# Four rounded weight blocks parked in DRAM: moving the splitting of the first right factors of a down projection into the attention part

## The chip, the cores and the metric

One core of a Trainium2 chip runs one launch of the kernel. The metric is the device time of that launch in microseconds (us), as a median over runs. A profiled execution gives the trace; its span is the time from its first to its last instruction on the engines.

## The reference

One encoder layer over 512 tokens of width 2048, all in float32:

```python
h = rms_norm(x, pre_mix_g);   z = h @ w_in                  # q | k | v | u
a = chunked_attention(q, k, v, rel_bias)                    # 8 heads of 128
p = multiscale_pool(u, pool_w, pool_scale)
x = x + rms_norm(concat(a, p) @ w_o, post_mix_g)
h = rms_norm(x, pre_ffn_g)
up = causal_dwconv(h @ w_up, conv_w, conv_b)                # w_up: 2048 x 2*5632
y = (gelu(up[..., :5632]) * up[..., 5632:]) @ w_down        # w_down: 5632 x 2048
x = x + rms_norm(y, post_ffn_g)
```

## The kernel before

**Numbers.** TensorE (PE) multiplies in a rounded format, fp32r. A factor that must be exact to more than that is *split*: ScalarE (ACT) writes a rounded copy, the high part (`hi`, L136), and VectorE (DVE) writes what is left, the low part (`lo`, L137). A product is then three matmuls, hi x hi, lo x hi and hi x lo (`mm3`, L152, L154, L155). In the trace `bh`, `bl` are the parts of a right factor, `ah`, `al` those of a left one, `p` the products.

**Stages.** The mixing part (queries, keys and values head by head, attention, pooling, `w_o`) takes the first third of the span. Weights come there through `load_w`, called by `Weights`: a raw tile from a ring of five (`raw4`), split into a pair from a ring of eight (`w4`, so four pairs), four blocks ahead of their use. `specs` is the list of blocks in the order of use. For each head h from 2 to 7 the loop does `head("q", h)`, `turn(h - 2)`, `scores(h - 1)`, `head("k", h)`, `values(h - 2)`. Between these steps `sums_in_dram` copies and adds blocks of `w_o` and `w_down` in DRAM (L284, L287), since both products are done by a seven-product scheme (Strassen's in Winograd's form) that multiplies sums of blocks.

Then comes the up projection, 22 pairs of column blocks (`u` from 0 to 21), the last 19 of them also with seven products each (`seven`, names `qa`, `qg`, `qd`). After each, DVE and ACT combine the products (`keep`, `keep_all`), apply the convolution (`taps`), the gelu (`gate`) and the product of the two halves (`product`), and the result goes to DRAM as `gd` (L916, L918), by a DMA that GpSimd (POOL) issues. `factors.order` fixes the order of the products; its end is written out by hand.

Last comes the down projection in five chunks plus a rest. A product there takes a right factor of 512 rows by 512 columns out of `w_down` or of a sum of its blocks, and a left factor out of `gd`: `multiply` issues 4 x 2 x 3 = 24 matmuls. The seven products are numbered 1 to 7 and each is done for two column halves, `cc` 0 and 1. For chunk 0 the order is `ORDER0`: (0,1), (1,1), (0,2), (1,2), then 5, 6, 3, 7, 4 for both halves.

**The passage.** So is called here the change from the up to the down projection. `right(c, cc)` is a generator that gives the split right factor of each product. In chunk 0 it loads one block (`first_right`, L845, issued by SyncE, SP; the names are `t` in the trace), from `w_down` for products 1, 2 and 3, from the sums in DRAM for the others, and splits it. `next_first` calls it for (0,1) and (1,1) while the up projection still runs; `factors()` (the second one, in the last part) gives all others, with their left factors (`left`, `gc` in the trace, L1197), and runs three products ahead of `multiply` (`AHEAD`).

The tiles of right factors are of 8 KB per partition. The first two of each kind (`right_tile`, tags `raw1`, `wh`, `wl`) lie in a pool `pr`, opened in place of the sums `h5`, `h3`, `h6`, which the last products of the up projection read. Later ones lie in a pool `p4` that takes the place of the up projection's tiles; the loop of `r("place")` fixes which ring lies where. A tile waits for the last reader of what lay there before.

**Order on the engines.** The order on PE is the program's own (`manual_schedule`). On ACT, DVE, POOL and SP a scheduler orders the instructions when the program is built, and then every engine takes them strictly in that order. `tc.issue_after(x)` places an instruction behind x.

Of the kernel before, what the change touches and what calls it, by code (L numbers as in the profile page):

```python
# [9 lines left out]
F32 = mybir.dt.float32  # L10
# [5 lines left out]
P = 128  # L16
S = 512
# [29 lines left out]
def f32(ap):  # L47
    return ap.bitcast(F32)
# [28 lines left out]
def encoder_layer(ctx: ExitStack, tc: tile.TileContext, x, xT, vecs, rel, post_mix, post_ffn,  # L77
# [56 lines left out]
    def split(hi, lo, src, scale=None):  # L134
        if scale is None:
            rounded = nc.scalar.activation(hi, src, AF.Copy)  # L136
            nc.vector.tensor_sub(lo, src, f32(hi))  # L137
        else:
            rounded = nc.scalar.activation(hi, src, AF.Copy, scale=scale)
            nc.vector.scalar_tensor_tensor(lo, src, scale, f32(hi), op0=ALU.mult, op1=ALU.subtract)  # L140
        split.last = rounded.ins
        return rounded.ins

    def load_w(name, src, a, b):
# [98 lines left out]
    def wo_specs(i, cc):  # L243
# [2 lines left out]
        return [(f"wo{i}_{cc}_{k}", whole[:, sl, :], 2, 512)  # L246
                for k, sl in enumerate(parts)]

    specs = v_specs(0)
    for h in range(1, HEADS):  # L250
        q, k = qk_specs(h)
        specs += q + k
        if h == 5:
            specs += v_specs(1)
    for g in range(4):
        for j in range(2):
            specs += halves(f"u{2 * g + j}", w_in, head_cols("u", 2 * g + j), 8, P)
        if g:
            specs += pm_spec(g - 1)
# [12 lines left out]


    first_sum = {i: [dram.tile([P, CU, S], F32, name=f"t{i}{cc}") for cc in range(2)] for i in (5, 7, 6, 4)}

    def first_block(cc, j, l):
        cs = slice(l * D // 2 + cc * S, l * D // 2 + (cc + 1) * S)
        return w_down[:2 * P * CU, cs].rearrange("(u j p) n -> p u j n", j=2, p=P)[:, :, j, :]

    def sums_in_dram():  # L280

# [61 lines left out]
    with tc.tile_pool(name="p1", bufs=2, reuse_waits="tile") as p1:  # L343
# [175 lines left out]
        for h in range(2, HEADS):  # L519
            head("q", h)  # L520
            next(sums_step)
            turn(h - 2)
            scores(h - 1)
            next(sums_step)
            head("k", h)
            next(sums_step)
            if h == 5:
                v_keep(1, v_group(1, lambda: values(3)))
            else:
                values(h - 2)  # L530
            next(sums_step)
        next(sums_step)
        pool_proj(0, 0)
# [274 lines left out]
    def right(c, cc):  # L808

        def load(j, l):  # L810
            b = later["raw2"](f"b{j}{l}") if j else raw1(f"b{j}{l}")
            r, cs = 256 * CU * c, slice(l * C + cc * S, l * C + (cc + 1) * S)
            nc.sync.dma_start(b, w_down[r:r + 256 * CU, cs].rearrange(
                "(u j p) n -> p u j n", j=2, p=P)[:, :, j, :])
            return b

        b = {}
        order = yield
        while True:
            i = order  # L820
            if c == 0:

                v = first_right(cc, i, raw1 if ORDER0.index((cc, i)) % 5 < 3 else later["raw2"])
            else:
                for jl in {1: (11, 12), 7: (22,), 2: (21,)}.get(i, ()):
                    b[jl] = load(jl // 10 - 1, jl % 10 - 1)
                if i == 5:
                    nc.vector.tensor_add(b[11], b[11], b[12])  # L828
                if i == 7:
                    nc.vector.tensor_add(b[12], b[22], b[12])  # L830
                if i == 6:
                    nc.vector.tensor_add(b[11], b[11], b[22])
                if i == 4:
                    nc.vector.tensor_add(b[21], b[21], b[11])
                v = b[{1: 11, 5: 11, 7: 12, 6: 11, 2: 21, 3: 22, 4: 21}[i]]
            hi, lo = right_tile("wh", "bh"), right_tile("wl", "bl")
            split(hi, lo, v)
            order = yield hi, lo

    def first_right(cc, i, ring):  # L840

        v = ring(f"t{i}")
        source = first_sum[i][cc] if i in first_sum else first_block(cc, *{1: (0, 0), 2: (1, 0), 3: (1, 1)}[i])
        with tc.issue_after(first_right.last) if first_right.last else nullcontext():
            first_right.last = nc.sync.dma_start(v, source).ins  # L845
        return v

    first_right.last = None

    ORDER = 1, 5, 7, 6, 2, 3, 4  # L850

# [36 lines left out]
    with tc.tile_pool(name="p3", bufs=2, reuse_waits="tile") as p3:  # L888
# [19 lines left out]

        def product(u, g, z):
            for j in range(2):  # L910
                c = p3.tile([P, S], F32, tag="cb", bufs=1, name="cb")
                taps(z[:, j, :], KF + 2 * u + j, c)
                nc.vector.tensor_mul(g[:, j, :], g[:, j, :], c)
            if u < NC * CU:
                for i in range(2):
                    nc.gpsimd.dma_start(gd[u // CU][i][:, u % CU, :, :], g[:, :, i * H:(i + 1) * H])  # L916
            else:
                nc.gpsimd.dma_start(gd_last[u - NC * CU], g)  # L918
# [85 lines left out]
        class Factors:  # L1004
# [20 lines left out]
            def load(self, k, i):  # L1025
                def raw(what, tile_, m, kh):
                    nc.sync.dma_start(tile_, self.block(k, m, kh))
                    self.raw[k, what] = tile_

                if i == 1:  # L1030
                    raw("w" if k in self.alone else "x", raw_x("wx"), 0, 0)
                elif i == 5 and k in self.alone:
                    raw("x", raw_x("wx"), 0, 0)
                    self.late.append((self.loaded + (2 if k else 0), k))
                elif i == 3:
                    raw("y", raw4("wy"), 1, 1)
                elif i == 2:
                    raw("z", raw4("wz"), 0, 1)
# [51 lines left out]
        def keep(k, i):  # L1090

            if i == 1:
                zs[k, "1"] = pair_tile("za", 1, 2)
                nc.scalar.activation(wide(zs[k, "1"]), banks[k, "a"], AF.Copy)
            elif i == 2:
                v = wide(zs[k, "1"])
                nc.vector.tensor_add(v, banks.pop((k, "d")), v)
            elif i == 5:
                zs[k, "5"] = raw_x("zb")[:, :S] if k == end else wide(pair_tile("zb", 1))
                nc.scalar.activation(zs[k, "5"], banks[k, "g"], AF.Copy)  # L1100
            elif i == 6:
                zs[k, "m"] = pair_tile("zm", 2)
                v = wide(zs[k, "m"][:, :1])
                nc.scalar.activation(v, banks[k, "a"], AF.Copy)  # L1104
                nc.vector.tensor_add(v, banks.pop((k, "g")), v)
            elif i == 7:
                v = wide(zs[k, "m"][:, 1:])
                keep.copied = nc.scalar.activation(v, banks[k, "a"], AF.Copy).ins
                nc.vector.tensor_add(v, zs.pop((k, "5")), v)
            elif i == 4:  # L1110
                keep_all(k)
# [50 lines left out]
        for k, i in factors.order:  # L1162
            seven(k, i)
            keep(k, i)
            if (k, i) == (end, 6):
                summed.close()
                pr = ctx.enter_context(tc.tile_pool(name="pr", bufs=2, side="right", reuse_waits="tile"))
            if (k, i) == (end, 6):
                next_first()
            elif (k, i) == (end, 7):  # L1170
                with tc.issue_after(keep.copied):
                    next_first()
        firsts = [multiply(l, r) for l, r in firsts]
    phase.close()

    with tc.tile_pool(name="p4", bufs=2, reuse_waits="tile") as p4:
# [10 lines left out]

        for r in (later["wh"], product_part, later["raw1"], half_g, raw2, later["wl"], slot_h, slot_l, scratch):  # L1190
            r("place")

        def left(c):

# [26 lines left out]
                i = yield hi, lo  # L1221

        def factors():
            nonlocal right_split
            for c in range(NC):
                ls, made = left(c), {}
                next(ls)
                rs = rights
                if c:
                    rs = [right(c, cc) for cc in range(2)]  # L1230
                    for r in rs:
                        next(r)
                order = [(cc, i) for cc, o in ((0, ORDER), (1, LAST if c == NC - 1 else ORDER)) for i in o]
                for cc, i in order if c else ORDER0[2:]:
                    r = rs[cc].send(i)
                    right_split = split.last
                    if i not in made:
                        made[i] = ls.send(i)
                    yield c, cc, i, made[i], r

        ready, right_split = [], None

        def next_product():
            c, cc, i, l, r = ready.pop(0)
# [2 lines left out]
        for f in factors():  # L1247
            ready.append(f)
            if firsts:
                with tc.issue_after(right_split), tc.issue_after(split.last):  # L1250
                    for cc, ps in enumerate(firsts):
                        keep_product(0, cc, 1, ps)
                firsts = ()
# [167 lines left out]
```

## Time and profile before

| what | value |
|---|---|
| time, median of 3 runs | 1887.79 us (1887.65 to 1889.65) |
| profiled execution, its own time | 1887.05 us |
| its span | 1885.0 us |
| PE busy | 1868.4 us, 99% of the span |
| DVE busy | 1423.7 us, 76% |
| ACT busy | 989.2 us, 52% |
| DMA | 410.24 MB, 218 GB/s over the span |
| end of the last up product on PE | about 1446 us after the start of the span |

In the views, a row of the timeline reads: start in us, length in us, engine, line, operation, out<-in, shapes, count; in brackets the idle time of the engine just before it and what ended that. A row of the waits reads: who waited for whom, us in total, times, longest. A row of the stretches reads: stretch, length, and for each engine the busy time with its number of instructions, then the granted clock of PE, the busy share of the 16 DMA engines and what they moved in GB/s. Ends of matmuls are modelled, and matmuls overlap: the distance of their starts tells their rate. Some matmul records are missing.

### The profile page before, as it was taken

The page shows a single profiled execution, that of the slowest core. Times are in us where ns is not written, and L with a number is a line of the kernel's source. Part 1 is how long each engine was busy: PE and PEld are TensorE (multiplying, and loading weights), DVE is VectorE, ACT ScalarE, POOL GpSimd, SP SyncE. Part 2 cuts the span into 40 slices and gives each one's busy share as a digit, 9 for nine tenths or more (in the row PEclk, how much of TensorE's full clock was granted, in tenths as well). Part 3 has the DMA queues.
Part 4 walks back from the last instruction along what each step waited for, and adds up shares of the span by engine and source line. Part 5 has one row for each costly group of instructions (what it writes and reads, how often), then busy time and mean ns, then how long its engine had stood idle before and what let it go on. Part 6 is the DMA issues. An engine that isn't in the chain of part 4 may idle for free.

```text
span 1885.0 us, 24700 instructions
## 1 busy us (share of the span) xinstructions
PE 1868.4 (99%) x9438; PEld 1594.3 (85%) x9438; DVE 1423.7 (76%) x1616; ACT 989.2 (52%) x1238; POOL 313.6 (17%) x403
## 2 busy tenths in 40 slices
PE   9999999999999999999999999999999999999998
PEld 7888888888888888888888888888887888888886
DVE  5454445587598667888888888888878799898877
ACT  6333233346465345656566566665656665465543
POOL 5101011000000102221222212122121122222221
PEclk9999999999999999999999999999999999999999
DMA  7599299359796848888888888888887999999998
GB/s 250 161 249 240 87 281 228 102 153 330 233 305 218 228 146 198 199 207 211 194 204 197 208 205 200 207 197 203 203 187 227 350 262 250 241 226 234 223 224 240
DMA packets 188230, 410.24 MB, mean 218 GB/s; under 512 B 11536, under 2 KB 62608, under 8 KB 183568
## 3 DMA queue, kind: packets, MB, share of 16 engines
q0 software_dynamic: 56384, 155.21, 44.0%
q1 hardware_dynamic: 131728, 253.46, 39.1%
q8 instruction: 74, 1.21, 0.3%
q14 instruction: 44, 0.36, 0.1%
HBM read 352.00 MB, written 106.95 MB: 243 GB/s over the span
## 4 chain that ended last, share of the span: by engine, by line
PE 94%; DVE 2%; DMA 1%; ACT 1%; issue 1%; SPq 0%; POOL 0%; POOLq 0%; DVEq 0%; ACTq 0%
PE qa L160 14%; PE qa L166 7%; PE qg L160 7%; PE p L155 6%; PE p L152 6%; PE p L154 6%; PE qg L166 4%; PE qd L160 3%; PE m L155 3%; PE m L152 3%; PE m L154 3%; PE up L154 2%; PE up L155 2%; PE up L152 2%; PE qd L166 2%; PE u L152 2%
## 5 line engine op out<-in xcount | busy, mean ns | idle before, releaser
L160 PE MATMUL qa<-gT,wfh 128*128 128x512 f32 x912 | 228.3, 392 | 0.0
L137 DVE TENSOR_TENSOR wfl<-wx,wfh 128x1024 fp32r<-128x1024 f32 x152 | 185.9, 1223 | 55.0 <-ACT wfh L136 40.1
L136 ACT ACTIVATE wfh<-wx 128x1024 fp32r<-128x1024 f32 x152 | 161.1, 1060 | 121.7 <-PE qg L160 46.4
L152 PE MATMUL p<-bh,ah 128*128 128x512 f32 x560 | 218.4, 390 | 1.3 <-ACT ah L136 1.3
L155 PE MATMUL p<-bh,al 128*128 128x512 f32 x560 | 218.7, 391 | 1.0 <-DVE al L137 1.0
L154 PE MATMUL p<-bl,ah 128*128 128x512 f32 x560 | 218.4, 390 | 1.2 <-DVE bl L137 1.2
L160 PEld LDWEIGHTS qa<-gT,wfh 128*128 128x128 f32 x912 | 164.1, 189 | 29.4
L1041 POOL DMA_DIRECT2D wx<-in_w_up x114 | 98.5, 864 | 452.8 <-DVE wfl L137 441.9
L160 PE MATMUL qg<-h,wfh 128*128 128x512 f32 x608 | 150.2, 389 | 0.0
L136 ACT ACTIVATE bh<-b 128x2048 fp32r<-128x2048 f32 x56 | 106.9, 1917 | 60.0 <-DVE b L828 39.3
L137 DVE TENSOR_TENSOR bl<-b,bh 128x2048 fp32r<-128x2048 f32 x56 | 127.6, 2287 | 9.0 <-PE p L154 8.0
L160 PEld LDWEIGHTS qg<-h,wfh 128*128 128x128 f32 x608 | 114.0, 188 | 23.5
L136 ACT ACTIVATE wfh<-wy 128x1024 fp32r<-128x1024 f32 x76 | 80.5, 1060 | 94.1 <-PE qg L160 46.2
L166 PE MATMUL qa<-gT,wfl 128*128 128x256 f32 x912 | 127.7, 283 | 1.2 <-ACT zm L1104 1.2
L155 PEld LDWEIGHTS p<-bh,al 128*128 128x128 f32 x560 | 105.5, 188 | 23.8 <-DVE al L137 1.8
L152 PEld LDWEIGHTS p<-bh,ah 128*128 128x128 f32 x560 | 105.5, 188 | 23.5 <-ACT ah L136 1.7
L154 PEld LDWEIGHTS p<-bl,ah 128*128 128x128 f32 x560 | 105.4, 188 | 23.3 <-DVE bl L137 1.6
L166 PEld LDWEIGHTS qa<-gT,wfl 128*128 128x128 f32 x912 | 119.9, 191 | 4.7 <-ACT zm L1104 1.6
L883 POOL DMA_DIRECT2D sum<-part x60 | 71.4, 1209 | 253.3 <-DVE part L874 114.3
L137 DVE TENSOR_TENSOR wfl<-wy,wfh 128x1024 fp32r<-128x1024 f32 x76 | 92.8, 1221 | 8.6 <-ACT wfh L136 4.7
L137 DVE TENSOR_TENSOR wfl<-wz,wfh 128x1024 fp32r<-128x1024 f32 x38 | 46.6, 1227 | 56.1 <-PE qa L160 51.9
L166 PEld LDWEIGHTS qg<-h,wfl 128*128 128x128 f32 x608 | 82.9, 190 | 5.9
(500 smaller groups left out, 4320.2 us busy)
## 6 DMA issues: line engine op xcount, KB each, us to landing
wx<-in_w_up POOLq DMA_DIRECT2D x114, 512.0 KB, 6.1
sum<-part POOLq DMA_DIRECT2D x70, 512.0 KB, 8.7
b<-in_w_down SPq DMA_DIRECT2D x32, 1024.0 KB, 9.3
wx<-in_w_up SPq DMA_DIRECT2D x40, 512.0 KB, 5.4
wz<-in_w_up SPq DMA_DIRECT2D x38, 512.0 KB, 5.7
wy<-in_w_up SPq DMA_DIRECT2D x38, 512.0 KB, 4.6
wy<-in_w_up POOLq DMA_DIRECT2D x38, 512.0 KB, 6.7
wt<-in_w_o POOLq DMA_DIRECT2D x16, 1024.0 KB, 11.5
```

The source lines that it names most:

```text
L136: rounded = nc.scalar.activation(hi, src, AF.Copy)
L137: nc.vector.tensor_sub(lo, src, f32(hi))
L152: nc.tensor.matmul(ps, l[0], r[0], start=first, stop=False)
L154: nc.tensor.matmul(low, l[0], r[1], start=False, stop=False)
L155: nc.tensor.matmul(ps, l[1], r[0], start=False, stop=last)
L160: nc.tensor.matmul(ps, w[0][:, kb], pairs[kb][0], start=fresh and not kb, stop=last, skip_group_check=not fresh)
L166: nc.tensor.matmul(ps[:, sl], w[1][:, kb], pair[:, sl], start=False, stop=last, skip_group_check=not fresh)
L883: nc.gpsimd.dma_start(dest, v, accum_op=ALU.add)
L1041: nc.gpsimd.dma_start(self.raw[k, what], self.block(k, m, kh), accum_op=ALU.add)
```

## The change

The right factors of the first four products of the down projection, (0,1), (1,1), (0,2) and (1,2), are plain blocks of `w_down`. They are now loaded and split in the mixing part, in heads 2, 3, 4 and 6, as two more blocks of 128 x 1024 in `specs` for each factor, and their high and low parts are written to DRAM by SP. At the passage `right` no longer loads and splits these four; POOL loads the two parts from DRAM straight into the tiles. The rest of the change orders the passage: the second of these requests is made earlier, the places of the rings in `p4` change, the splits for products 5 and 6 are placed behind the first left split, and the last `product` uses a second scratch tile (`cx`), so that its two halves no longer share one.

```diff
@@ split
-            nc.vector.tensor_sub(lo, src, f32(hi))
+            rest = nc.vector.tensor_sub(lo, src, f32(hi))
...
-        split.last = rounded.ins
+        split.last, split.rest = rounded.ins, rest.ins
@@ encoder_layer
+    READY = {2: (0, 1), 3: (1, 1), 4: (0, 2), 6: (1, 2)}
+    ready_w = {at: [dram.tile([P, CU, S], F32, name=f"rw{at[0]}{at[1]}{p}") for p in "hl"] for at in READY.values()}
+
+    def ready_specs(h):
+        if h not in READY:
+            return []
+        cc, i = READY[h]
+        return [(f"rw{cc}{i}_{j}", first_block(cc, i - 1, 0)[:, 2 * j:2 * j + 2, :], 2, 512) for j in range(CU // 2)]
+
     specs = v_specs(0)
     for h in range(1, HEADS):
         q, k = qk_specs(h)
         specs += q + k
         if h == 5:
             specs += v_specs(1)
+        specs += ready_specs(h)
@@ the loop over heads
                 values(h - 2)
+            for j in range(CU // 2 if h in READY else 0):
+                cc, i = READY[h]
+                for dest, v in zip(ready_w[cc, i], weights.get(f"rw{cc}{i}_{j}")):
+                    nc.sync.dma_start(dest[:, 2 * j:2 * j + 2, :], f32(v))
             next(sums_step)
@@ right
             i = order
+            if (c, (cc, i)) in ready_first:
+                hi, lo = right_tile("wh", "bh"), right_tile("wl", "bl")
+                for v, source in zip((hi, lo), ready_w[cc, i]):
+                    nc.gpsimd.dma_start(v, source.bitcast(F32R))
+                order = yield hi, lo
+                continue
             if c == 0:
-                v = first_right(cc, i, raw1 if ORDER0.index((cc, i)) % 5 < 3 else later["raw2"])
+                v = first_right(cc, i, raw1 if (ORDER0.index((cc, i)) - len(ready_first)) % 5 < 3 else later["raw2"])
@@ first_right
-        source = first_sum[i][cc] if i in first_sum else first_block(cc, *{1: (0, 0), 2: (1, 0), 3: (1, 1)}[i])
+        source = first_sum[i][cc] if i in first_sum else first_block(cc, 1, 1)
...
+    ready_first = [(0, at) for at in READY.values()]
@@ product
-                c = p3.tile([P, S], F32, tag="cb", bufs=1, name="cb")
+                if u == NU - 1 and j:
+                    c = raw_x("cx")[:, :S]
+                else:
+                    c = p3.tile([P, S], F32, tag="cb", bufs=1, name="cb")
@@ Factors.load
-                    self.late.append((self.loaded + (2 if k else 0), k))
+                    self.late.append((self.loaded + (3 if k else 0), k))
@@ the loop over factors.order
             if (k, i) == (end, 6):
                 next_first()
-            elif (k, i) == (end, 7):
-                with tc.issue_after(keep.copied):
-                    next_first()
+            elif (k, i) == (end - 1, 4):
+                next_first()
@@ the places of p4
-        for r in (later["wh"], product_part, later["raw1"], half_g, raw2, later["wl"], slot_h, slot_l, scratch):
+        for r in (product_part, later["raw1"], later["wh"], half_g, raw2, later["wl"], slot_h, slot_l, scratch):
             r("place")
+        for _ in range(3):
+            slot_l("place")
@@ factors
-                    r = rs[cc].send(i)
-                    right_split = split.last
+                    with ExitStack() as behind:
+                        if c == 0 and i in (5, 6):
+                            for ins in first_split:
+                                behind.enter_context(tc.issue_after(ins))
+                        r = rs[cc].send(i)
+                    if (c, cc, i) == (0, 1, 2):
+                        first_split = split.last, split.rest
...
             if firsts:
-                with tc.issue_after(right_split), tc.issue_after(split.last):
+                with tc.issue_after(split.last):
                     for cc, ps in enumerate(firsts):
                         keep_product(0, cc, 1, ps)
```

In the built program the order on PE is the same before and after, matmul for matmul. On POOL the end of the order is now: the last additions to `wx`, the next to last `gd`, high and low part of (0,1), high and low part of (1,1), the low part of (1,2), the last `gd`, high and low part of (0,2), the high part of (1,2), and then the writes of the products' sums. The low part of (1,2) has the tile of the low part of (0,1), and so waits for the second to last matmul of the first product; the other three tiles are free before the up projection's last product. On SP the passage now has: the sums for (0,5) and (1,5), the two `gc` blocks, the sums for (0,6) and (1,6), the block for (0,3), and so on.

More of the change, by code (lines that the diff above doesn't have):

```diff
@@ L136, in split @@
             rounded = nc.scalar.activation(hi, src, AF.Copy)
-            nc.vector.tensor_sub(lo, src, f32(hi))
+            rest = nc.vector.tensor_sub(lo, src, f32(hi))
         else:
             rounded = nc.scalar.activation(hi, src, AF.Copy, scale=scale)
-            nc.vector.scalar_tensor_tensor(lo, src, scale, f32(hi), op0=ALU.mult, op1=ALU.subtract)
-        split.last = rounded.ins
+            rest = nc.vector.scalar_tensor_tensor(lo, src, scale, f32(hi), op0=ALU.mult, op1=ALU.subtract)
+        split.last, split.rest = rounded.ins, rest.ins
         return rounded.ins
@@ L247, in wo_specs, with first_block @@
                 for k, sl in enumerate(parts)]
+    def first_block(cc, j, l):
+        cs = slice(l * D // 2 + cc * S, l * D // 2 + (cc + 1) * S)
+        return w_down[:2 * P * CU, cs].rearrange("(u j p) n -> p u j n", j=2, p=P)[:, :, j, :]
+    READY = {2: (0, 1), 3: (1, 1), 4: (0, 2), 6: (1, 2)}
[5 more added lines that the diff above has]
+        return [(f"rw{cc}{i}_{j}", first_block(cc, i - 1, 0)[:, 2 * j:2 * j + 2, :], 2, 512) for j in range(CU // 2)]
     specs = v_specs(0)
@@ L274, in encoder_layer @@
     first_sum = {i: [dram.tile([P, CU, S], F32, name=f"t{i}{cc}") for cc in range(2)] for i in (5, 7, 6, 4)}
-    def first_block(cc, j, l):
-        cs = slice(l * D // 2 + cc * S, l * D // 2 + (cc + 1) * S)
-        return w_down[:2 * P * CU, cs].rearrange("(u j p) n -> p u j n", j=2, p=P)[:, :, j, :]
     def sums_in_dram():
@@ L1107, in keep @@
                 v = wide(zs[k, "m"][:, 1:])
-                keep.copied = nc.scalar.activation(v, banks[k, "a"], AF.Copy).ins
+                nc.scalar.activation(v, banks[k, "a"], AF.Copy)
                 nc.vector.tensor_add(v, zs.pop((k, "5")), v)
@@ L1223, in factors @@
         def factors():
-            nonlocal right_split
             for c in range(NC):
@@ L1239, in factors @@
                     yield c, cc, i, made[i], r
-        ready, right_split = [], None
+        ready = []
         def next_product():
```

## The prediction

> **What bounds the kernel now.** First the page's busy times, then the same by stage.
>
> ```profile
> PE 1868.4 (99%) x9438; PEld 1594.3 (85%) x9438; DVE 1423.7 (76%) x1616; ACT 989.2 (52%) x1238; POOL 313.6 (17%) x403
> ...
> 100.00:350.00 250.00, 250.00 (x1193) 210.73 (x1192) 122.77 (x232) 83.49 (x153) 21.46 (x47) 1.00 0.80 209
> ...
> 1490.00:1860.00 370.00, 370.00 (x1634) 306.46 (x1633) 323.98 (x231) 195.95 (x189) 77.56 (x67) 1.00 0.97 244
> ```
>
> PE is the bound: idle for 16.6 of 1885 us, never in the heads (100 to 350 us) and never in the down projection behind the passage (1490 to 1860). So work spared on ACT or DVE is worth nothing except where PE waits for it, and a stall added is paid in full. The waits of PE show where it waits in the passage, and its timeline shows how much is lost there:
>
> ```profile
> PE p L152 <- ACT ah L136: 1.3, 1, 1.3
> PE p L154 <- DVE bl L137: 1.2, 1, 1.2
> PE p L155 <- DVE al L137: 1.0, 2, 0.6
> ...
> 1445.94 0.39 PE L152 MATMUL p<-bh,ah 128*128 128x512 f32 x1
> ...
> 1456.59 0.39 PE L155 MATMUL p<-bh,al 128*128 128x512 f32 x1
> 1458.30 0.50 PE L152 MATMUL p<-bh,ah 128*128 128x512 f32 x1 [1.32 <-ACT ah L136]
> 1460.05 0.50 PE L154 MATMUL p<-bl,ah 128*128 128x512 f32 x1 [1.25 <-DVE bl L137]
> 1461.19 0.80 PE L155 MATMUL p<-bh,al 128*128 128x512 f32 x1 [0.63 <-DVE al L137]
> ...
> 1464.22 0.39 PE L152 MATMUL p<-bh,ah 128*128 128x512 f32 x1
> ...
> 1474.66 0.39 PE L154 MATMUL p<-bl,ah 128*128 128x512 f32 x1
> ```
>
> The first down product starts at 1445.94. From there to 1456.59 are 47 steps (two products of 24 matmuls), 0.2266 us each. The matmul at 1474.66 is the second in the second triple of the fifth product, so 4 x 24 + 4 = 100 steps from the start: undisturbed it would stand at 1445.94 + 22.66 = 1468.60. **The passage loses 6.06 us.** That is all that the change can win; what follows runs without a gap.
>
> **What it removes.** Two groups of rows carry the passage on the two helpers:
>
> ```profile
> 1440.57 2.29 DVE L137 TENSOR_TENSOR bl<-t,bh 128x2048 fp32r<-128x2048 f32 x1
> ...
> 1450.21 1.23 DVE L1120 TENSOR_TENSOR z<-z,RR 128x1024 f32<-128x1024 f32 x1
> 1452.32 0.75 DVE L893 SCALAR_TENSOR_TENSOR cb<-z,vec,cb 128x511 f32<-128x511 f32 x1 [0.89 <-ACT cb L892]
> ...
> 1457.10 0.69 DVE L913 TENSOR_TENSOR ca<-ca,cb 128x512 f32<-128x512 f32 x1
> ...
> 1446.56 0.36 ACT L1118 ACTIVATE z<-qa 128x256 f32<-128x256 f32 x1
> 1451.47 0.82 ACT L892 ACTIVATE cb<-z,vec 128x512 f32<-128x512 f32 x1 [4.54 <-DVE z L1120]
> 1455.40 1.90 ACT L136 ACTIVATE bh<-t 128x2048 fp32r<-128x2048 f32 x1
> ```
>
> Four splits go: 4 x 1.90 on ACT, 4 x 2.29 on DVE. Two of DVE's stand ahead of the last `z` (1450.21), so `z` can start right behind ACT's copy, at 1446.92. Then `z` 1.23, the first `cb` 0.82, and on DVE, with `cx` so that the halves overlap, 4 x 0.75 + 2 x 0.69: the last product of halves ends at 1446.92 + 1.23 + 0.82 + 3.00 + 1.38 = 1453.35, against 1457.79 now. By itself this would free the third product's left factor in time, and the 6 us with it.
>
> **What it adds at the passage.** The third and fourth product now wait for POOL's queue. Its rows, and SP's:
>
> ```profile
> 1427.11 0.57 POOL L918 DMA_DIRECT2D gd<-ca  x1 [0.42 <-DVE z L1116]
> 1458.35 0.55 POOL L918 DMA_DIRECT2D gd<-ca  x1 [30.67 <-ACT ah L136]
> 1459.50 0.72 POOL L885 DMA_DIRECT2D sum<-part  x1 [0.61 <-ACT part L878]
> ...
> 1446.13 0.34 SPq L1197 DMA_DIRECT2D gc<-gd  x1
> 1446.57 0.37 SPq L845 DMA_DIRECT2D t<-in_w_down  x1
> 1447.05 0.44 SPq L845 DMA_DIRECT2D t<-t  x1
> 1447.58 0.51 SPq L1197 DMA_DIRECT2D gc<-gd  x1
> 1448.19 0.92 SPq L845 DMA_DIRECT2D t<-t  x2
> ```
>
> POOL issues the loads for (0,1) and (1,1) behind the `gd` of 1427.11, from 1427.7 on: their tiles are free by then, and the first product starts 18 us later. The next in POOL's order, the low part of (1,2), waits for the first product's end, 1451.4, and behind it stands the last `gd`, which cannot go before 1453.35 + 0.56 (the distance from DVE's end at 1457.79 to 1458.35 now) = 1453.9. Only then comes the high part of (0,2). With 0.55 for `gd` and 0.72 for a load, (0,2) is requested at 1454.5 (high) and 1455.2 (low). Its tiles have been free since 1440; it waits in line. The third product should start at 1445.94 + 48 x 0.2266 = 1456.82, and its second matmul reads the low part.
>
> When do these parts land? The page of SP's requests, each of 1 MB:
>
> ```profile
> DMA to landing us min/median/max: 4.9/4.9/4.9
> DMA to landing us min/median/max: 8.3/13.9/19.2
> ...
> 1457.00:1461.00 4.00, 1.01 (x2) 0.37 (x2) 3.97 (x4) 4.00 (x7) 1.78 (x3) 0.96 1.01 426
> q1 hardware_dynamic: 222, 1.56, 74.1%
> q0 software_dynamic: 149, 0.55, 26.8%
> ```
>
> The first line is the `gc` of 1446.13, which found the DMA engines empty. The second is the four `t` issued right behind it, up to 1448.67: they land up to 19.2 us after issue, one after the other, with the engines full (share 1.01 at 426 GB/s in the third line). The last two are SP's and POOL's queue from 1461 to 1466 us: they share those engines, 74% and 27%. The changed kernel still sends 5 MB on SP's queue at 1446 to 1448 (two `gc`, two `t` for product 6, one for product 3). On POOL's queue, ahead of the end of (0,2)'s low part, come the low part of (1,2), `gd`, and the two parts: 1.05 + 0.52 + 2 x 1.05 = 3.67 MB. Together 8.9 MB; 1.3 of them are through by 1451 (251 GB/s in 1446 to 1451, as now), the rest takes 7.6 / 0.426 = 18 us: 1469. Bounds: alone on the engines from 1454.5, (0,2)'s high part lands after 4.9 and the low part 2.5 (1.05 MB at 426) later, 1462; with a quarter of the engines until SP is through, 1475. I take 1469.5, as both queues are known to be full then.
>
> So the third product's second matmul comes at 1469.5 instead of 1457.05: 12.5 us. The clock adds to it: after the pause now, 1461.19 to 1464.22 holds 8 steps in place of 13.4, 1.2 us lost, and I take 1.7 after a longer one. Then (1,2)'s high part (3 us behind) and the splits for product 5 are ready, since DVE and ACT had the pause for them. Loss 14.2 in place of 6.06: **+8.1 us at the passage**, and nothing behind it gives that back.
>
> The Trainium skill speaks against the change here: "DMA: Bandwidth & Descriptors", section "Issuing engines are not separate DMA queues", says that a second issuing engine brings no bandwidth, as all use the same 16 DMA engines. The two shares above, 101% together, agree.
>
> **What it adds in the heads.** Eight loads and 16 writes of 0.5 MB, and 8 splits. Prices, from the page and the DMA view of 95 to 135 us:
>
> ```profile
> L137 DVE TENSOR_TENSOR wfl<-wx,wfh 128x1024 fp32r<-128x1024 f32 x152 | 185.9, 1223 | 55.0 <-ACT wfh L136 40.1
> L136 ACT ACTIVATE wfh<-wx 128x1024 fp32r<-128x1024 f32 x152 | 161.1, 1060 | 121.7 <-PE qg L160 46.4
> k_0r<-in_w_in SPq DMA_DIRECT2D x1, 512.0 KB, 16.7
> ```
>
> DVE gets 8 x 1.22 = 9.8 us more in stretches where it is busy half of the time, ACT 8.5. A load stands five raw tiles and four pairs, nine blocks, ahead of its use. With six blocks a head instead of four, that is 1.5 heads; the two projections of a head alone are 96 steps, 21.8 us, so the lead is over 32 us against a landing of 16.7 at worst and 2.3 for the split. SP's queue is passed by 16 writes that wait for splits; behind them stand weights of the next head, with the same lead. The tighter place is the split of the next head's first query block, which now gets its pair only half a projection (5.4 us) plus `values` before its use: 2.3 of 5.4 needed. I count 0; were it late by its whole 2.3 in four heads, 9.
>
> The later `late` step leaves POOL's order as it was: 0. The new order for products 5 and 6 only moves work under the pause: 0.
>
> **The sum.** The profiled execution took 1887.05 (span 1885.0 and 2.05 around it), 0.7 under the median. 0 + 8.1 on it is 1895.2; on the median, **1896 us**.
>
> **Rivals.** (1) *No change*: the loads meet idle DMA engines and land at the lower bound, 1462: loss 5.0 + 1.2 = 6.2, time 1888. It needs SP's 5 MB to be out of the way, and they are issued at 1446. The Trainium skill's fit for one POOL request ("DMA: Bandwidth & Descriptors", "Anatomy of one DMA — SWDGE (gpsimd) path": 2.0 us plus the bytes at 436 GB/s) gives 4.4 us for 1 MB, and as an estimate by that page the same end; it is for a lone request. (2) *Faster*: (0,2) arrives by 1457 and the 6.06 us are won, 1882. It needs POOL to issue it before 1452, ahead of a `gd` that is not computed until 1453; only a much earlier DVE chain could do that. (3) *Far slower*: POOL's loads land as slowly as its additions do:
>
> ```profile
> wt<-in_w_o POOLq DMA_DIRECT2D x16, 1024.0 KB, 11.5
> ...
> gd<-ca POOLq DMA_DIRECT2D x1, 512.0 KB, 7.7
> ```
>
> Taken one behind the other at half that, 5.6 us per MB, from 1434.8 (the `gd` of 1427.11 plus 7.7), seven parts and a `gd` are through at 1477: 8 us more than forecast, 1904, and the second product waits too, for (1,1)'s low part. (4) *The heads stall*: query blocks late as priced above, up to 9 us more: 1905.
>
> **Chances.** Forecast 0.57, rival 1 0.13, rival 2 0.10, rival 3 0.12, rival 4 0.08. A measurement can tell about 0.2%, 3.8 us, from no change: faster 0.10, same 0.13, slower 0.77. The range takes in the lower bound and stops short of the far ends of rivals 3 and 4: 1888 to 1904.
>
> **What would show it.** Right: in the profile after, POOL's load for (0,2) starts at about 1454.5 behind a `gd`, the third product's first two matmuls wait for DMA `bh` and `bl` for some 12 us, the granted clock drops there, and 100 to 350 us still has PE at 250.00. Wrong: the load's start before 1452, a landing by 1462, or waits of PE on `q` blocks. A third product on time at 1456.8 would overturn the forecast.

## The result: slower, by almost four times the forecast

The changed kernel takes 1918.92 us (median of 5 runs, 1914.75 to 1922.52) against 1887.79 (5 runs, 1887.13 to 1891.03). The ratio is 1.0159, with a 95% interval of 1.0139 to 1.0179: some 30 us more, 26 to 34. Forecast was 1896, with a range to 1904. The sign was right; the size was not.

The profiled execution of the changed kernel took 1920.83 us. The head of its page:

```profile
span 1919.1 us, 24753 instructions
PE 1876.5 (98%) x9438; PEld 1599.3 (83%) x9438; DVE 1420.7 (74%) x1620; ACT 989.2 (52%) x1242; POOL 318.1 (17%) x411
```

Its stretches (length, busy time of PE, PEld, DVE, ACT and POOL, then granted clock, DMA share, GB/s):

```profile
100.00:350.00 250.00, 238.62 (x1122) 199.70 (x1121) 120.48 (x224) 85.45 (x152) 21.34 (x44) 0.98 0.93 251
...
1525.00:1860.00 335.00, 332.71 (x1461) 275.03 (x1460) 295.63 (x195) 181.41 (x164) 70.32 (x61) 0.99 0.96 231
```

DVE and ACT are hardly busier than before. PE now idles for 11.4 us in the heads, where it had no gap, and 2.3 us early in the down projection, where it had none either. Its waits say for whom:

```profile
PE p L152 <- DMA bh<-rw02h: 11.3, 1, 11.3
PE a L152 <- ACT pth L136: 7.3, 1, 7.3
PE q L155 <- DVE q_0l L137: 3.0, 2, 1.8
PE qa L166 <- ACT zm L1128: 2.7, 1, 2.7
PE p L154 <- DMA bl<-rw02l: 2.4, 1, 2.4
PE p L154 <- DVE bl L137: 2.3, 1, 2.3
```

Two of these are the forecast's (`rw02h`, `rw02l`); the others are not. As PE does the same 9438 matmuls in the same order in both kernels, the n-th of one can be set against the n-th of the other. The lag of the changed kernel grows here:

| where | lag grows by |
|---|---|
| ahead of the 600th matmul | 0.2 us |
| heads, 600th to 1500th | 14.9 us |
| start of the up projection | 1.5 us |
| last products of the up projection, at `zm` | 3.1 us |
| the passage, to its fifth product | 10.0 us |
| first chunk to second in the down projection | 4.2 us |
| the rest | 0.0 us |

Together 33.8 us in these two profiled executions. The largest part, 14.9 us, lies in the heads, where the forecast had counted nothing.

**The heads.** ACT's timeline there:

```profile
166.02 0.75 ACT L136 ACTIVATE pth<-pt 128x384 fp32r<-128x384 f32 x2
185.74 1.06 ACT L136 ACTIVATE q_0h<-q_0r 128x1024 fp32r<-128x1024 f32 x1 [18.96 <-issue]
186.70 0.26 ACT L136 ACTIVATE pth<-pt 128x128 fp32r<-128x128 f32 x1
```

SP's timeline, where the first half of (0,2) goes to DRAM:

```profile
165.12 1.33 SPq L544 DMA_DIRECT2D rw02h<-rw_0h  x1
```

The DMA issues of SP, with KB and us from issue to landing:

```profile
rw02h<-rw_0h SPq DMA_DIRECT2D x1, 512.0 KB, 20.5
rw02l<-rw_0l SPq DMA_DIRECT2D x1, 512.0 KB, 21.2
q_0r<-in_w_in SPq DMA_DIRECT2D x1, 512.0 KB, 10.5
```

In the built program the split of `q_0h`, for head 5, writes the tile that holds the high part of (0,2)'s first half, and so waits for the write of that part to DRAM. The write is issued at 165.12 and lands 20.5 us later, at 185.6. The split starts at 185.74: "issue" stands here for a DMA that the profile does not name. It is not the load of the query block: that was issued at 155.37 and landed at 165.8, 20 us earlier. Behind it on ACT, in order, stands the last `pth`, and for that PE waits 7.3 us to finish `values`. DVE's low part of the query follows late too. ACT's waits show the same for two earlier blocks, by name and at little cost to PE (one wait of 1.2 us for a low part of the query block behind):

```profile
ACT rw_1h L136 <- DMA rw11h<-rw_0h: 12.1, 1, 12.1
...
ACT rw_1h L136 <- DMA rw01h<-rw_0h: 10.1, 1, 10.1
```

While these writes are under way the DMA engines are full, and PE's clock falls; first the changed kernel, then the kernel before:

```profile
175.00:200.00 25.00, 14.82 (x56) 11.33 (x55) 6.79 (x18) 5.22 (x11) 1.81 (x5) 0.80 1.08 285
```

```profile
175.00:200.00 25.00, 25.00 (x124) 21.22 (x123) 13.05 (x26) 9.69 (x19) 0.58 (x4) 1.00 0.44 121
```

The DMA share is 1.08 in place of 0.44, and the clock averages 0.80. A write of the same size that the same execution issued at 145.90, with a DMA share of 0.83 from 143 to 149 us, landed after 2.6 us. Of the 14.9 us, the waits of PE at `a` and at `q` make 11.7 (7.3, 3.0, 1.0 and 0.4); the other 3.2 go with the slower clock behind them (0.72 from 186 to 200 us).

**The passage.** POOL's timeline:

```profile
1471.23 0.53 POOL L838 DMA_DIRECT2D bl<-rw12l  x1 [21.79 <-PE p L155]
1473.27 0.54 POOL L942 DMA_DIRECT2D gd<-ca  x1 [1.50 <-ACT part L899]
1473.80 0.54 POOL L838 DMA_DIRECT2D bh<-rw02h  x1
1474.32 0.55 POOL L838 DMA_DIRECT2D bl<-rw02l  x1
```

The two issues, with us to landing:

```profile
bh<-rw02h POOLq DMA_DIRECT2D x1, 1024.0 KB, 14.0
bl<-rw02l POOLq DMA_DIRECT2D x1, 1024.0 KB, 16.7
```

PE's timeline, the first and the third product:

```profile
1465.56 0.39 PE L152 MATMUL p<-bh,ah 128*128 128x512 f32 x1
...
1487.89 0.77 PE L152 MATMUL p<-bh,ah 128*128 128x512 f32 x1 [11.29 <-DMA bh<-rw02h]
1491.07 0.80 PE L154 MATMUL p<-bl,ah 128*128 128x512 f32 x1 [2.42 <-DMA bl<-rw02l]
```

The first product starts at 1465.56, 19.6 us later than before. With that shift added, the forecast's steps stand so: low part of (1,2) at 1471.0 (measured 1471.23), `gd` at 1473.5 (1473.27), high part of (0,2) at 1474.1 (1473.80), low part landed at 1489.1 (1491.03). The third product's second matmul comes 14.4 us late; 12.5 was forecast. The clock drops in this pause:

```profile
1475.00:1494.00 19.00, 5.29 (x16) 3.62 (x15) 4.65 (x3) 5.73 (x5) 1.85 (x3) 0.65 1.04 395
```

**Between the first two chunks.** PE waits 2.3 us for `bl` there, and the matmuls behind that start 0.43 us apart for a while, in place of 0.23. The low part is late because DVE is; DVE's timeline, and one of POOL's issues with us to landing:

```profile
1560.19 1.29 DVE L895 TENSOR_TENSOR part<-p,part 128x512 f32<-128x512 f32 x2 [5.12 <-issue]
...
sum<-part POOLq DMA_DIRECT2D x1, 512.0 KB, 12.2
```

This write was issued at 1547.91 and landed at 1560.11, and DVE's addition started 0.08 us later. In the built program an addition of this kind writes a `part` tile that an earlier write to DRAM reads. So it is the fault of the heads once more, on another engine. In the kernel before, the write landed at 1524.11 and the addition followed at 1524.25 without a wait.

### The profile page after: what moved, and what is told of

Same layout as the page of the kernel before. It is cut to its first block, busy times and chain, and to the rows that moved or that the text cites. A ratio compares the mean times of both kernels' runs of the same rounds, so it can differ in the third digit from the quotient of the medians.

```text
span 1919.1 us, 24753 instructions
## 1 busy us (share of the span) xinstructions
PE 1876.5 (98%) x9438; PEld 1599.3 (83%) x9438; DVE 1420.7 (74%) x1620; ACT 989.2 (52%) x1242; POOL 318.1 (17%) x411
## 4 chain that ended last, share of the span: by engine, by line
PE 89%; DMA 5%; DVE 2%; ACT 1%; issue 1%; SPq 1%; POOL 0%; DVEq 0%; ACTq 0%; POOLq 0%
PE qa L160 14%; PE qa L166 7%; PE qg L160 7%; PE p L154 6%; PE p L155 6%; PE p L152 6%; PE qg L166 4%; PE qd L160 3%; PE m L155 3%; PE m L152 3%; PE m L154 2%; PE up L154 2%; PE up L155 2%; PE up L152 2%; PE qd L166 2%; PE u L155 2%
## 5 line engine op out<-in xcount | busy, mean ns | idle before, releaser
L152 PEld LDWEIGHTS p<-bh,ah 128*128 128x128 f32 x560 | 106.0, 189 | 34.0 <-issue 11.7
```

The costliest lines, as they stand in the source:

```text
L152: nc.tensor.matmul(ps, l[0], r[0], start=first, stop=False)
```

## The experiments

Each ratio is to the kernel before, with its 95% interval, from interleaved runs on one chip: one chip for the first four experiments (the kernel before took 1889.93 us there), another for the rest (1889.09). Four questions were open: what the heads lose, why, whether the order on POOL makes the pause, and whether anything in the change is a gain.

### Only the work in the heads: heads_alone

```diff
 (the kernel before)
+    READY = {2: (0, 1), 3: (1, 1), 4: (0, 2), 6: (1, 2)}
...
+        specs += ready_specs(h)
...
+            for j in range(CU // 2 if h in READY else 0):
+                cc, i = READY[h]
+                for dest, v in zip(ready_w[cc, i], weights.get(f"rw{cc}{i}_{j}")):
+                    nc.sync.dma_start(dest[:, 2 * j:2 * j + 2, :], f32(v))
```

> The kernel before, with only the work in the heads added: four blocks loaded, split, and both parts written to DRAM; the passage is as before and nothing reads the parts. Theory A (a pair of the ring is not free until its write to DRAM has landed, ACT waits in its split for that, and everything behind it on ACT waits too): 1888 + 15 = 1903 us, the split of a query block starts when the write of a high part lands, after some 19 us of waiting, and PE waits about 7 us for pth. Rival B (the prediction's zero: the heads hide it, and what the changed kernel lost there came from something else in it): 1888 us, PE busy 250.00 from 100 to 350 us.

Measured: 1905.94 us, ratio 1.0087 (1.0074 to 1.0101). ACT's timeline:

```profile
188.61 1.06 ACT L136 ACTIVATE q_0h<-q_0r 128x1024 fp32r<-128x1024 f32 x1 [18.41 <-issue]
```

PE's waits:

```profile
PE a L152 <- ACT pth L136: 6.8, 1, 6.8
PE q L155 <- DVE q_0l L137: 4.2, 2, 2.4
```

The stretch of the heads:

```profile
100.00:350.00 250.00, 239.03 (x1111) 199.59 (x1110) 118.53 (x221) 85.98 (x153) 21.37 (x44) 0.97 0.93 249
```

The stall is there without the rest of the change, at the same split and of the same length. It costs about 16 us by itself. Rival B falls.

### The same traffic without a held pair: no_hold

```diff
-                for dest, v in zip(ready_w[cc, i], weights.get(f"rw{cc}{i}_{j}")):
-                    nc.sync.dma_start(dest[:, 2 * j:2 * j + 2, :], f32(v))
+                weights.get(f"rw{cc}{i}_{j}")
+                for dest in ready_w[cc, i]:
+                    nc.sync.dma_start(dest[:, 2 * j:2 * j + 2, :], first_block(cc, i - 1, 0)[:, 2 * j:2 * j + 2, :])
```

> The changed kernel, with each of the 16 writes in the heads replaced by a copy of as many bytes from the weight matrix in DRAM to the same place, issued at the same point of SP's order; the loads and splits stay. So the traffic stays and no pair of the ring is held by a write. The stored parts are then the raw block twice, so the products of four right factors are others. Theory A (held pairs): the 15 us of the heads go, 1919 - 15 = 1904 us, PE idle under 3 us from 100 to 350 us with the DMA share still about 0.9. Rival C (the bytes themselves make weights late): 1919 us, PE still idle for 11 us there.

Measured: 1906.83 us, ratio 1.0097 (1.008 to 1.0113). The stretch of the heads:

```profile
100.00:350.00 250.00, 249.41 (x1189) 210.06 (x1188) 136.27 (x251) 95.71 (x170) 23.03 (x52) 1.00 0.89 232
```

PE's waits:

```profile
PE p L152 <- DMA bh<-rw02h: 11.0, 1, 11.0
PE p L154 <- DVE bl L137: 3.2, 1, 3.2
```

The DMA engines are nearly as full (0.89), and PE loses 0.6 us in the stretch in place of 11.4. So it is the held pair, not the bytes. The copies also no longer wait for the splits on SP, so that the loads behind them can go earlier; but the load of the stalled query block had landed 20 us before its split, so late loads do not explain the stall. The passage keeps its whole pause, as theory A wants. By medians the heads alone cost 16 us and this kernel 17, together 33, where the whole change cost 31.

### Another order on POOL: queue_order

```diff
-                nc.gpsimd.dma_start(gd_last[u - NC * CU], g)
+                (nc.scalar if u == NU - 1 else nc.gpsimd).dma_start(gd_last[u - NC * CU], g)
...
-                for v, source in zip((hi, lo), ready_w[cc, i]):
-                    nc.gpsimd.dma_start(v, source.bitcast(F32R))
+                with tc.issue_after(right.last) if (cc, i) == (1, 2) else nullcontext():
+                    for v, source in zip((hi, lo), ready_w[cc, i]):
+                        right.last = nc.gpsimd.dma_start(v, source.bitcast(F32R)).ins
...
-            if firsts:
+            if len(ready) > 1 and firsts:
```

> The changed kernel with another order on POOL: the last gd is issued by ACT instead, the requests for (1,2) stand behind those for (0,2), low part of (1,2) last. Theory D (the parts of (0,2) wait in line): they are requested at about 1458 instead of 1474, land before the third product needs them at 1476, and the third product's pause of 11.3 + 2.4 us goes; a few us come back at the low part of (1,2), which still waits for the first product's end: 1919 - 10 = 1909 us, 1905 to 1912. Rival E (the DMA engines are full from 1450 to 1494 us, and an earlier request only pushes other transfers back): another part, gc or t is late by as much, within 4 us of 1919.

Measured: 1906.62 us (4 runs), ratio 1.0093 (1.0079 to 1.0107). POOL's timeline:

```profile
1457.84 0.54 POOL L839 DMA_DIRECT2D bh<-rw02h  x1 [11.01 <-PE qa L160]
1458.36 0.54 POOL L839 DMA_DIRECT2D bl<-rw02l  x1
...
1468.62 0.53 POOL L839 DMA_DIRECT2D bl<-rw12l  x1 [9.20 <-PE p L155]
```

PE's timeline, the start of the third product:

```profile
1474.56 0.50 PE L152 MATMUL p<-bh,ah 128*128 128x512 f32 x1 [0.57 <-ACT ah L136]
```

PE's waits from 1440 to 1560 us:

```profile
PE p L154 <- DMA bl<-rw12l: 4.0, 1, 4.0
PE p L152 <- ACT ah L136: 0.6, 1, 0.6
PE p L155 <- DVE al L137: 0.5, 1, 0.5
```

Requested 16 us earlier (13 us, counted from the start of the first product), (0,2) no longer holds the third product up. The wait moves to the fourth, for the one part whose tile is not free until the first product ends: 4.0 us. The passage loses 2.7 us more than before instead of 10.0, and the 4.2 us between the first two chunks are gone as well (`bl` is not among these waits), while no_hold still loses 4.8 there. So they go with the pause: DVE's addition waits for its `part` tile here too, but 3.2 us in place of 5.1, and PE is covered. The Trainium skill's "DMA: Bandwidth & Descriptors", section "Issuing engines are not separate DMA queues", says that all issuers share the same 16 DMA engines. The trace agrees: the share of the 16 engines was 1.04 from 1457 to 1475 us, and the parts of (0,2) still took 11.2 and 15.9 us to land. What helped was the place in line.

### Two blocks ready in place of four: two_ready

```diff
-    READY = {2: (0, 1), 3: (1, 1), 4: (0, 2), 6: (1, 2)}
+    READY = {2: (0, 1), 3: (1, 1)}
...
-        source = first_sum[i][cc] if i in first_sum else first_block(cc, 1, 1)
+        source = first_sum[i][cc] if i in first_sum else first_block(cc, *{2: (1, 0), 3: (1, 1)}[i])
```

> The changed kernel with only (0,1) and (1,1) made ready in heads 2 and 3; (0,2) and (1,2) are loaded and split at the passage again. Theories A and D: head 4 has no write, so of the 15 us only the 1.4 us of head 3 are left; POOL's queue holds nothing that the third product needs; the passage costs no more than before (two splits of four go): 1888 + 1.5 - 1 = about 1889 us, 1884 to 1894. Rival F (POOL's loads and the new order cost the passage some 10 us however many they are): 1900 us.

Measured: 1890.54 us (11 runs), ratio 1.0007 (0.9998 to 1.0016). Its profiled execution, 1895.2 us, is the slowest of the eleven. Matched against before, its passage wins 4.5 us of the 6.06, and its heads lose 7.6 us. (Another 2.4 us are lost in the first 50 us, before any block is made ready, and are not put down to the change.) In the heads 1.4 us fall at head 3, as expected; the other 6.2 were not expected. They follow a like wait on another engine. POOL's timeline:

```profile
179.22 1.24 POOL L297 DMA_DIRECT2D wt<-in_w_o  x1 [11.01 <-DMA wt<-in_w_o]
187.24 1.24 POOL L297 DMA_DIRECT2D wt<-in_w_o  x1 [6.79 <-DMA wt<-in_w_o]
187.98 0.74 POOL L442 MEMSET s<- 64x64 f32 x2
```

DVE's timeline:

```profile
188.67 0.29 DVE L444 TENSOR_REDUCE nm<-s 128x1 f32<-128x128 f32 x1 [17.23 <-POOL s L442]
```

POOL's additions wait for SP's copies of `w_o`, and the DMA share is 1.09 or more from 160 to 200 us, where the kernel before has 0.31 from 180 to 190. A short memset for the scores stands behind them, and DVE waits 17.2 us for that. Rival F falls: with two blocks the passage is faster than before.

### The two blocks where the DMA engines are free: two_quiet, and without the second scratch tile

```diff
-            specs += v_specs(1)
-        specs += ready_specs(h)
+            specs += v_ready_specs()
... (v_specs(1), with a ready block behind its blocks 0, 2, 4 and 5)
+                if i and c in READY_AT:
+                    (cc, n), j = READY_AT[c]
+                    for dest, v in zip(ready_w[cc, n], weights.get(f"rw{cc}{n}_{j}")):
+                        nc.sync.dma_start(dest[:, 2 * j:2 * j + 2, :], f32(v))
```

> As two_ready, but the four blocks of (0,1) and (1,1) are loaded, split and written between the eight blocks of the second value projection, behind its blocks 0, 2, 4 and 5, where the DMA engines were busy 0.28 to 0.73 of the time. Theory A (a pair is held as long as its write takes): the writes land in some 3 us there, less than the 5.4 us between two blocks, and nothing stalls; the passage keeps what two_ready won there, 4.5 us: 1888 - 4.5 = about 1884 us, below the kernel before. Rival G (the heads pay for every block made ready, wherever it stands): two_ready's 10 us in its profiled run come back in part, 1888 to 1893 us.

The second run takes the second scratch tile (`cx`) out again:

> As two_quiet, without the second scratch tile in the last product. If the shorter chain on DVE (cx) carries a part of the passage's gain, the last product of halves is some 1.2 us later and so are the splits behind it: 1885 to 1886 us. If the two splits that are gone carry all of it: 1884 us.

Measured: two_quiet 1884.1 us (11 runs, 1882.43 to 1887.36), ratio 0.9975 (0.9966 to 0.9984); without the second scratch tile 1886.91 us, ratio 0.9987 (0.9979 to 0.9996). The first is faster than the kernel before, by some 4.7 us. Its heads:

```profile
100.00:350.00 250.00, 250.00 (x1193) 210.73 (x1192) 127.76 (x236) 87.65 (x157) 21.46 (x47) 1.00 0.88 235
```

Two of its writes, with us to landing:

```profile
rw11h<-rw_0h SPq DMA_DIRECT2D x1, 512.0 KB, 2.6
rw11l<-rw_0l SPq DMA_DIRECT2D x1, 512.0 KB, 3.4
```

PE's timeline, its only wait in the passage:

```profile
1459.16 0.50 PE L155 MATMUL p<-bh,al 128*128 128x512 f32 x1 [1.26 <-DVE al L137]
```

A write of the same size lands in 2.6 us here, against 20.5 in head 4 of the changed kernel, and PE loses nothing. (Six of the eight writes land in 2.6 to 3.4 us, the last two in 6.5 and 7.2.) Rival G falls. Without the second scratch tile the wait for `al` is 2.5 us, and the passage wins 1.4 us in place of 4.5. So the second scratch tile counts; so does the rest of the change at the passage, two splits fewer and the new order taken together.

### The second scratch tile alone, and a second look at the kernel before

```diff
 (the kernel before)
+                if u == NU - 1 and j:
+                    c = raw_x("cx")[:, :S]
```

> The kernel before with only the second scratch tile. The chain z, cb, ca on DVE ends 1.2 us earlier (4 x 0.75 + 2 x 0.69 behind the first cb), and the three waits at the third product (1.3, 1.25, 0.63) shrink by as much: 1887 us. If the splits on DVE ahead of z decide, nothing: 1888 us. Either is within what a measurement tells from no change; the waits in the profile decide.

> The kernel before, for a second profile of it. All changed kernels so far lose 1.3 to 1.5 us more than before at the zm of the last products (start 1387 us in the profile before), also the one whose passage is untouched. If that is a matter of the run, this profile shows a wait of 1.2 to 2.7 us there too and another time; if it belongs to the changes, 1.2 us as before.

Measured: cx_alone 1887.38 us, ratio 0.9992 (0.9983 to 1.0001), not to be told from no change by its time. In its trace the passage wins 1.2 us, as worked out, but not in the way expected: the wait for `ah` (1.3 us before) is gone, those for `bl` and `al` are no shorter (1.4 and 1.0). In the passage the second scratch tile alone wins 1.2 us and the rest without it 1.4; together they win 4.5. The second profile of the kernel before took 1891.55 us, with no change in it. Its waits of PE:

```profile
PE qa L166 <- ACT zm L1104: 3.5, 1, 3.5
PE p L152 <- ACT ah L136: 1.3, 1, 1.3
PE p L154 <- DVE bl L137: 1.3, 1, 1.3
```

The wait for `zm` was 1.2 us in its first profile and is 3.5 here, and its matmuls fall back by 3.9 us at that place. So the 3.1 us that the changed kernel lost there are within what the run alone can do, and are not put down to the change.

## Why the prediction was right in the passage and wrong in the sum

**The passage: right.** The order on POOL, the moment of each request, the wait of the third product and the lower clock (0.65 from 1475 to 1494 us) came as forecast, 19.6 us later; the loss there grew by 10.0 us where 8.1 stood. The difference is the landing of (0,2)'s low part: 16.7 us after its request, 14.3 forecast. queue_order shows the cause that was named: with the request moved ahead of `gd` and of (1,2), the pause at the third product went. That something would also be late between the chunks behind the passage (4.2 us) was missed: the prediction says only that "nothing behind it gives that back", and counts no further cost there.

**The heads: wrong, and this is the step that failed.** "I count 0" has two halves. The first is the lead of the loads, and it held where it could be seen: the load of the stalled query block had landed 20 us before its split. The second is "the split of the next head's first query block", which the prediction named as the tighter place, with "2.3 of 5.4 needed". That takes the block's pair to be free in time and sets only the length of the split against the room. It holds for a pair that PE reads, which is free when the product is done. A block made ready is read by a DMA, and its pair is free when the write has landed: 20.5 us after its issue, so that ACT waited 19.0 us to begin the split. The prediction named the 16 writes only as something that SP's queue is passed by, and gave their landing no price, although its own rows had a load of 0.5 MB at 16.7 us in that stage. Nor did it ask what stands behind the split on ACT: `pth`, for which PE waited 7.3 us. Rival 4 had the right place, with up to 9 us, but priced it by the split's own length (2.3 us in four heads); the mechanism was another, and 14.9 us were lost. no_hold, with as many bytes written and no held pair, loses 0.6 us of PE in that stretch. That the landing time matters too is shown by two_quiet: the hold is harmless where a write takes 3 to 7 us.

**What stays open.** The other two terms put at 0, the `late` step and the order for products 5 and 6, show no cost of their own in any run, but they were not run alone. The 1.5 us at the start of the up projection appear in heads_alone too (1.1), and cx_alone lost 0.5 there; their cause is left open.

**Rival 2** ("(0,2) arrives by 1457") named what a gain needs, but tied it to an earlier chain on DVE. Two other ways were found. queue_order brought (0,2) in time by the order on POOL, though its passage still lost 2.7 us, now for (1,2). two_ready and two_quiet won 4.5 us of the 6.06 by not storing (0,2) and (1,2) at all.

## What to carry to other kernels

In these traces a tile that a DMA reads is not written again until that DMA has landed, and the time to landing went with the load on the DMA engines: for the same 0.5 MB, in one execution, 2.6 us at a DMA share of 0.83 and 20.5 at 1.11. So for each write added out of a ring, look up who takes the tile next, on which in-order engine it waits, and what stands behind it there. Work moved out of a tight place needs a place with slack in every resource that it touches; by their ratios (1.0007 and 0.9975) the same two blocks made 6 us of difference, depending on where in the heads they were made ready. A mean over a stage does not show such a place: in the kernel before, the DMA share of the heads is 0.80 on average, but 1.10 from 140 to 160 us and 0.31 from 180 to 190.

## What the runs showed that was not expected

Equal writes of the changed kernel, issued 19 us apart in one execution (145.90 and 165.12), differed eightfold in landing: 2.6 and 20.5 us. And one unlabelled "issue" of 19.0 us was the longest of ACT's waits in the heads: the profile names no DMA there, so the landing times had to be set beside it.
